# One Griffin/PEER decoder layer on one core: the mixers in two passes of 160 and 384 columns instead of one of 544

## The chip, the core and the metric

The kernel runs on one core of a Trainium2 chip. The metric is the device time of one execution in microseconds (us). Five engines take part: TensorE (PE, with its weight loads shown apart as PEld), VectorE (DVE), ScalarE (ACT), GpSimd (POOL) and SyncE (SP, which only issues DMAs). Each works through its own instructions in their order and waits at semaphores for the others.

## The reference

One layer is computed for 512 prompt tokens and 8 sequences of 4 sampled tokens, 544 tokens in all, with width 2048, in float32.

```python
def decoder_layer(x, ple, ...):
    n1 = rmsnorm(x, norm_mix)
    xr, gr, q, k, v, ga, gb = split(n1 @ w_in)            # 2048 -> 7680 columns
    xr, conv_new = causal_conv(xr, conv_buf, conv_w, conv_b)
    hr, h_last = rglru(xr, h0, ...)                        # linear recurrence over the tokens
    branch_a = (hr * gelu(gr)) @ w_proj_rnn
    o = attention over a window of 128 keys, with sinks    # q, k normed and rotated
    branch_b = o @ w_proj_attn
    x = x + (sigmoid(ga) * branch_a + sigmoid(gb) * branch_b) @ w_out
    x = x + peer(rmsnorm(x, norm_ffn), w_peer_q, peer_sub_keys, peer_u, peer_v)
    x = x + (ple @ w_ple) * sigmoid(rmsnorm(x, norm_ple) @ w_ple_gate)

def peer(x, w_q, sub_keys, u, v):     # 16384 experts, 8 heads, 16 experts of each head
    s = scores of (x @ w_q) against 2 x 128 sub-keys per head
    idx, g = softmax of the 16 best sums of the two top-16 lists
    h = gelu(x . u[idx]) * g
    return sum over the 128 chosen experts of h * v[idx]
```

A prompt token's recurrence and attention read only earlier prompt tokens; a sampled token reads only its own sequence's cache and state.

## The kernel before

Activations lie with the model dimension on the 128 partitions and tokens along the row: sixteen tiles of 128 x 544. A matmul has 128 x 128 weights and streams the tokens' columns. The work is a list of *units*: one unit is one 512 KB block of weights (8 tiles of 128 x 128). SP loads it (`wr`), ACT rounds it to a high part `wh` (line 230), DVE computes the rest `wl` (line 231), and PE multiplies, for each of the 8 tiles, `wh` by the high and the low part of the activations and `wl` by the high part: 24 products, each with a weight load of its own. With 544 columns each product is two matmuls of 272 columns (line 290), 48 matmuls a unit; with 384 columns it is one (line 286), 24 a unit.

The units come in this order: 4 for `w_ple`; the **mixers**, 120 for `w_in`, 32 for the two projections, 32 for `w_out`, 32 for `w_pq`, all with 544 columns (216 units); 256 for `u` and 256 for `v` with 384 columns; 32 for `w_gate` with 544.

PEER is done in two ways. The first 384 prompt tokens are done **densely**: all 16384 experts are multiplied (stages U and V), with a gate matrix `Gd` that is zero for experts not chosen. It is built in stage U: `tk1` and `tk2` find the top 16 on DVE, then `place` makes gate tiles with f16 matmuls (line 996) that ACT writes out (lines 1001, 1003). The other 160 tokens, the last prompt block and the samples, are done **sparsely**: their experts' rows are fetched by indirect DMAs issued on POOL (line 1076), 160 of `u` and 160 of `v`, 1 MB each, and DVE does a dot product (line 1089) or a scaled addition (line 1097) with each.

Such side work lives in generators that `side()` advances twice per unit, at a pace that the `PACE_...` constants set; so all engines' orders are fixed when the program is built. Some places call `drain()`, which issues all that is left of them at once. One is `gates_done`, 24 units before the end of stage U, where the gate matrix has to be complete: all that stage U's pace has not yet issued of `tk1`, `tk2` and `place` is put there, ahead of the next unit.

Of the kernel before, what the change touches and what calls it, by code (L numbers as in the profile page):

```python
# [17 lines left out]
P = 128  # L18
# [6 lines left out]
LP = 568  # L25
LH = LP // 2
RN = 8
# [3 lines left out]
NS = P + NSB  # L31
# [12 lines left out]
PACE_U, PACE_V = (1.3, 0.36), (1e6, 0.40)  # L44
NWA = min(NW - 4, 2 * KT * T // (2 * DC))
# [12 lines left out]
TT = _token_tiles(DC, T) + _token_tiles(0, DC)  # L58
# [10 lines left out]
def _build(ctx, tc, nc, I, O):  # L69
# [16 lines left out]
    xr_t = [None] * KT  # L86
    rawf = act.tile([P, KT * T], F32, name="raw")
    raw = rawf.rearrange("p (k t) -> p k t", k=KT)
    opf = act.tile([P, 2 * KT * T], F32R, name="opf")
    misc = act.tile([P, KT * NS + 3 * DC], F32, name="misc")  # L90
# [5 lines left out]
    ident = const("ident", [P, P])  # L96


    AH, AL = [None] * KT, [None] * KT

    def act_tile(k):
        return opf[:, 2 * k * T:(2 * k + 1) * T], opf[:, (2 * k + 1) * T:(2 * k + 2) * T]
# [17 lines left out]
    def sq_add(k, pool, x=0):  # L120

        new = x not in ssum
        if new:
            ssum[x] = 0, T, misc[:, (4 + x) * T:(5 + x) * T]
        s = ssum[x][2] if new else pool.tile([P, T], F32, name="sq", tag=f"sq{x}", bufs=2 - x)
        if x:
            GP.tensor_mul(s, raw[:, k, :], raw[:, k, :])
        else:
            A.activation(s, raw[:, k, :], AF.Square)
        if not new:  # L130
            (GP if x else V).tensor_add(ssum[x][2], ssum[x][2], s)

    def make_rs(keep):
        yield
        ps = psum.tile([P, 2, 512], F32, name="aux", tag="aux", bufs=2)
        for s in range(2):
            lo, hi = s * HB, (s + 1) * HB
            cut = sorted({lo, hi} | {c for c0, c1, _ in ssum.values() for c in (c0, c1) if lo < c < hi})
            for x, y in zip(cut, cut[1:]):
                qs = [q[:, x - c0:y - c0] for c0, c1, q in ssum.values() if c0 <= x and y <= c1]  # L140
# [4 lines left out]
        rs = keep[0] = cst.tile([P, T], F32, name="rs", tag="rs", bufs=1)  # L145
        A.activation(two(rs), ps[:, :, :HB], AF.Sqrt, bias=eps_t, scale=1.0 / D)
        V.reciprocal(rs, rs)


    LOADA, SPLITA = 4, 2  # L150
    pace = dict(main=1e6, sp=0.0)
    owed = dict(main=0.0, sp=0.0)

    def side():

        SPS["tick"] = SPS.get("tick", 0) + 1
        owed["sp"] += pace["sp"]
# [4 lines left out]
        while owed["main"] > 0:  # L162
            c, more = advance()
            owed["main"] -= c
            if not more:
                break

# [7 lines left out]
    def gemm(src, ops, epi, nk=2, cols=None, **kw):  # L175

        key = object()
        for hc in range(nk):
            last = hc == nk - 1
            unit(src(hc), [(key, [(kl, (lambda k=hc * 8 + kl: ops(k))) for kl in range(8)], hc == 0, last,  # L180
# [35 lines left out]
    def run_units():  # L216
        rawt, hit, lot = {}, {}, {}
        n = len(units)

        def load(u):  # L220
            if u < n:
                rawt[u] = wgt.tile([P, 8, P], F32, name="wr", tag="wr", bufs=3)
                SP.dma_start(out=rawt[u], in_=units[u]["src"])
# [9 lines left out]
        for u in range(LOADA):  # L233
            for k in ((0, 4, 8, 12) if u == LOADA - 1 else ()):
                SP.dma_start(out=raw[:, k:k + 4, :], in_=I["xT"][k:k + 4].rearrange("k p t -> p k t"))
                if k == 0:
                    load(u)
            if u < LOADA - 1:
                load(u)
        for u in range(SPLITA):  # L240
            split(u)
        for u in range(n):
# [5 lines left out]
            load(u + LOADA)  # L248
# [53 lines left out]
    def act_ops(k):  # L302
        return AH[k], AL[k]


    pa = ExitStack()
    pG = pa.enter_context(tc.tile_pool(name="pG", bufs=1))
    pA = None
    pl = ExitStack()
    pL = pl.enter_context(tc.tile_pool(name="pL", bufs=1))  # L310

    def aconst(pool, name, shape):
        t = pool.tile(shape, F32, name=name)
        SP.dma_start(out=t, in_=I[name])
        return t

    rs1 = [None]

    def start_a():
        for _ in range(N0A):  # L320
            yield
        for k in range(KT):
            AH[k], AL[k] = act_tile(k)
            split_to(AH[k], AL[k], raw[:, k, :], gn[:, 0, k:k + 1])
            if k < NPS:
                sq_add(k, pL, 1)
# [1179 lines left out]
```

## Time and profile before

| | us |
|---|---|
| median of 3 runs (4072.27 to 4082.82) | 4072.59 |
| profiled execution, its time | 4068.44 |
| its span, first to last instruction | 4066.6 |
| PE busy in the span | 3917.9 |
| DVE busy | 2694.7 |
| ACT busy | 1300.6 |
| POOL busy | 535.9 |

The profiled execution's own time is 1.84 us above its span. PE is busy for 96% of the span, but the end of a matmul is modelled and neighbours overlap, so this share does not say how fast the matmuls follow each other; that is read from the starts in the timeline or from a piece of the chain with its count. The granted TensorE clock is 0.979 of full speed as a mean.

### The profile page before, as it was taken

The numbers are of one execution on the slowest core, as the hardware profiler recorded it, in microseconds if no ns is written. First come the engines' busy times: TensorE is split into PE (matmuls) and PEld (weight loads), VectorE is DVE, ScalarE is ACT, GpSimd is POOL, SyncE is SP. The second block draws the span as 40 slices with busy tenths as digits, with TensorE's granted clock in tenths as the row PEclk, the third lists the DMA queues.
The fourth block names the chain that finished last, engine by engine and source line by source line (L and its number), as shares of the span: only waits on it lengthen the run. The fifth ranks groups of instructions, "written<-read, shape, count | busy, mean of one in ns | idle before, by whom it ended". The sixth has DMA issues, their size and how long they took to land.

```text
span 4066.6 us, 62629 instructions
## 1 busy us (share of the span) xinstructions
PE 3917.9 (96%) x26069; PEld 3847.3 (95%) x26069; DVE 2694.7 (66%) x3782; ACT 1300.6 (32%) x1653; POOL 535.9 (13%) x486
## 2 busy tenths in 40 slices
PE   7999999999999999999999998289999999999999
PEld 7999999999999999999999998289999999999999
DVE  7765445333434348998788987857788889578543
ACT  4442344421223223333333233133222323233421
POOL 3000000000000001222222221001222222013000
PEclk9999999999999999999999999599999999999999
DMA  5232232234333336998999998268999999689342
GB/s 189 79 113 95 74 101 92 93 101 147 131 130 116 114 110 228 332 334 325 335 339 327 332 331 316 90 228 314 345 366 383 362 358 376 234 283 365 124 136 99
DMA packets 324620, 909.47 MB, mean 224 GB/s; under 512 B 27496, under 2 KB 163624, under 8 KB 283248
## 3 DMA queue, kind: packets, MB, share of 16 engines
q1 hardware_dynamic: 201008, 489.54, 35.2%
q0 software_dynamic: 54400, 363.36, 23.5%
q10 hardware_dynamic: 68928, 52.57, 3.9%
q8 instruction: 204, 3.34, 0.3%
q14 instruction: 80, 0.66, 0.0%
HBM read 824.74 MB, written 80.63 MB: 223 GB/s over the span
## 4 chain that ended last, share of the span: by engine, by line
PE 72%; DVE 14%; DMA 8%; issue 3%; ACT 2%; SPq 1%; ACTq 1%; POOL 0%; DVEq 0%; POOLq 0%
PE acc L290 37%; PE acc L286 30%; DMA wr<-i_v 6%; DVE wl L231 4%; DVE raw L1097 2%; ACT wh L230 1%; DVE raw L1089 1%; DMA Gd<-gst 1%; PE aux L996 1%; DVE gb L1089 1%; ACTq L1150 1%; SPq L1178 1%; PE aux L525 1%; PE aux L562 1%; DVE gt L1182 0%
## 5 line engine op out<-in xcount | busy, mean ns | idle before, releaser
L286 PE MATMUL acc<-opf,wh 128*128 128x384 f32 x7424 | 1903.8, 337 | 4.2 <-ACT wh L230 4.1
L231 DVE TENSOR_TENSOR wl<-wr,wh 128x1024 fp32r<-128x1024 f32 x764 | 933.9, 1223 | 1175.7 <-ACT wh L230 1166.9
L290 PE MATMUL acc<-opf,wh 128*128 128x272 f32 x7936 | 1341.1, 291 | 22.9 <-ACT wh L230 9.7
L230 ACT ACTIVATE wh<-wr 128x1024 fp32r<-128x1024 f32 x764 | 804.9, 1059 | 1698.2 <-PE acc L290 772.3
L286 PEld LDWEIGHTS acc<-opf,wh 128*128 128x128 f32 x7424 | 1340.8, 188 | 7.2 <-ACT wh L230 7.2
L286 PE MATMUL acc<-opf,wl 128*128 128x384 f32 x3712 | 1247.5, 336 | 9.2 <-DVE wl L231 8.9
L290 PEld LDWEIGHTS acc<-opf,wh 128*128 128x128 f32 x7936 | 1132.7, 189 | 36.5 <-issue 14.1
L290 PE MATMUL acc<-opf,wl 128*128 128x272 f32 x3968 | 823.8, 289 | 0.0
L286 PEld LDWEIGHTS acc<-opf,wl 128*128 128x128 f32 x3712 | 697.7, 188 | 17.2 <-DVE wl L231 16.9
L290 PEld LDWEIGHTS acc<-opf,wl 128*128 128x128 f32 x3968 | 622.9, 189 | 0.3 <-DVE wl L231 0.3
L1097 DVE SCALAR_TENSOR_TENSOR raw<-gb,hsp,raw 128x2048 f32<-128x2048 f32 x96 | 225.0, 2343 | 1.8 <-DMA gb<-i_vn,idx 1.8
L1089 DVE SCALAR_TENSOR_TENSOR raw<-raw,misc 128x2048 f32<-128x2048 f32 x95 | 216.7, 2281 | 0.0
L1076 POOL DMA_INDIRECT raw<-i_un,idx x95 | 140.7, 1481 | 485.9 <-DVE raw L1097 274.0
L286 PE MATMUL acc<-wx,wh 128*128 128x384 f32 x768 | 196.9, 337 | 5.8 <-ACT wh L230 5.7
L1076 POOL DMA_INDIRECT gb<-i_vn,idx x97 | 128.7, 1326 | 539.8 <-DVE gb L1089 389.0
L1149 ACT ACTIVATE misc<-misc 128x384 f32<-128x384 f32 x128 | 67.4, 526 | 404.4 <-DVE misc L1148 404.4
L1089 DVE SCALAR_TENSOR_TENSOR gb<-gb,misc 128x2048 f32<-128x2048 f32 x65 | 148.3, 2282 | 0.0
L286 PEld LDWEIGHTS acc<-wx,wh 128*128 128x128 f32 x768 | 139.4, 189 | 7.4 <-ACT wh L230 7.4
L1097 DVE SCALAR_TENSOR_TENSOR raw<-raw,hsp 128x2048 f32<-128x2048 f32 x62 | 145.3, 2343 | 0.0
L1076 POOL DMA_INDIRECT gb<-i_un,idx x65 | 81.6, 1255 | 478.3 <-DVE raw L1097 240.5
L286 PE MATMUL acc<-wx,wl 128*128 128x384 f32 x384 | 130.3, 339 | 4.1 <-DVE wl L231 3.9
L1076 POOL DMA_INDIRECT raw<-i_vn,idx x63 | 87.2, 1383 | 286.2 <-DVE raw L1089 272.6
(302 smaller groups left out, 2316.4 us busy)
## 6 DMA issues: line engine op xcount, KB each, us to landing
wr<-i_u SPq DMA_DIRECT2D x256, 512.0 KB
wr<-i_v SPq DMA_DIRECT2D x256, 512.0 KB
wr<-i_w_in SPq DMA_DIRECT2D x120, 512.0 KB
Hd<-misc ACTq DMA_DIRECT2D x128, 192.0 KB
Gd<-gst ACTq DMA_DIRECT2D x12, 2048.0 KB
gt<-Gd SPq DMA_DIRECT2D x32, 768.0 KB
misc<-Hd SPq DMA_DIRECT2D x112, 192.0 KB
wr<-i_w_proj SPq DMA_DIRECT2D x32, 512.0 KB
```

Source lines behind the costliest of these rows:

```text
L230: A.activation(hit[u], r, AF.Copy)
L231: V.tensor_sub(lot[u], r, hit[u].bitcast(F32))
L286: PE.matmul(acc[:, 0, :ncol], lhsT=w[:, kl, :], rhs=x[:, :ncol], start=st and t == 0, stop=sp and t == 2)
L290: PE.matmul(acc[:, s, :HB], lhsT=w[:, kl, :], rhs=x[:, s * HB:(s + 1) * HB], start=st and t == 0, stop=sp and t == 2)
L525: PE.matmul(sc[:, g, j0:], lhsT=raw[hs, RN + 4 * kp + g, blk * P:(blk + 1) * P], rhs=Q["k", kp][hs, ks:ks + nk], start=True, stop=True)
L562: PE.matmul(ps[hs, 0, :], lhsT=Q["v", kp][:, blk - 1 + kb, hs], rhs=pt[:, kb, :], start=kb == kbs[0], stop=kb == 1)
L996: PE.matmul(pq[:, q], lhsT=oo[:, q // 2, 0, :, q % 2], rhs=gl[:, q // 2, x, :, q % 2], start=x == 0, stop=x == 1)
L1076: GP.indirect_dma_start(out=t, out_offset=None, in_=I[kind + "n"], in_offset=bass.IndirectOffsetOnAxis(ap=idx[:, i:i + 1], axis=0))
L1089: V.scalar_tensor_tensor(t, t, 1.0, xtok, op0=ALU.mult, op1=ALU.mult, accum_out=hsp[:, i:i + 1])
L1097: V.scalar_tensor_tensor(vacc, t, hsp[:, i:i + 1], vacc, op0=ALU.mult, op1=ALU.add)
L1149: A.activation(h, h, AF.Gelu_apprx_tanh)
L1150: A.dma_start(out=Hd[e], in_=h)
```

## The change

The tokens are put in the order: prompt blocks 1 to 3 (384 columns), prompt block 0 (128), samples (32). The 216 mixer units are run twice. **Pass A** does prompt block 0 and the samples, 160 columns; **pass B** does blocks 1 to 3, 384 columns, with the keys, values, convolution rows and recurrence state of block 0 kept from pass A. Each pass has its 216 units of weights loaded, split and multiplied, 24 matmuls a unit. The sparse tokens are now those of pass A. Their top-16 work runs as a background generator (`bg`) during the end of pass A and the start of pass B, and the rows of their experts are fetched during pass B and stage U (`u` rows) and during stages U and V (`v` rows; a `v` row may be fetched once pass B's scores are done). Stage U's side work keeps only the top-16 work and the placing of the three dense blocks. In pass A the weights of `w_in` are loaded into a ring of six buffers in memory that pass B's activations use later. Stages U, V and `w_gate` have the same matmuls as before.

```diff
-NS = P + NSB
+NA = P + NSB
+DB = T - NA
+NC = 0
+NS = NA + NC
 DC = T - NS
...
-PACE_U, PACE_V = (1.3, 0.36), (1e6, 0.40)
-NWA = min(NW - 4, 2 * KT * T // (2 * DC))
+PACE_A, PACE_U, PACE_V = 0.26, (1.35, 0.27), (1e6, 0.38)
+PACE_T = 1.2
...
-TT = _token_tiles(DC, T) + _token_tiles(0, DC)
+TT = _token_tiles(DB, T) + _token_tiles(DC, DB) + _token_tiles(0, DC)
+TA = 2
+TS = len(TT) - len(_token_tiles(0, DC))
...
+    PA, PB_ = Pass(), Pass()
+    for S, c0, n, npr, blk, ns, lp in ((PA, DB, NA, P, 0, NSB, 184), (PB_, 0, DB, DB, 1, 0, DB)):
+        S.c0, S.n, S.npr, S.blk, S.ns, S.lp = c0, n, npr, blk, ns, lp
...
+        def load():
+            u = nld[0]
+            if units[u].get("ring"):
+                r = u % RING
+                rawt[u] = rawf[:, r * 1024:(r + 1) * 1024].rearrange("p (k m) -> p k m", k=8)
+            else:
+                rawt[u] = wgt.tile([P, 8, P], F32, name="wr", tag="wr", bufs=WRB)
+            SP.dma_start(out=rawt[u], in_=units[u]["src"])
...
+    def split_b():
+        for k in range(8):
+            split_raw(PB_, (k,), 0)
+            yield
...
+        def win(epi):
+            gemm(wsrc("w_in", c[0]), S.ops, epi, cols=S.n)
...
+        for n in range(RN):
+            win(lambda a, n=n: (epi_xr(S, n, a), gens.append(lru(S, n))))
+            win(lambda a, n=n: epi_gr(S, n, a))
...
+        def post_lru():
+            flush()
+            drain()
+            if S is PB_:
+                while bg:
+                    bg_step()
...
+                X["t"] = [pX.tile([P, D], F32, name=f"xr{i}") for i in range(2)]
+                SPS["slots"] = SPS["slots"] + X["t"]
...
+            if S is PA:
+                open_l(PB_)
+                lru_consts(PB_)
+                TP["st"] = ExitStack()
+                TP["p"] = TP["st"].enter_context(tc.tile_pool(name="pT", bufs=1))
+                TP.update(eq=1, w=32, skl=None, sc=None)
+                pace.update(bg=PACE_T)
+                gens.append(rs_and_x())
+                return
...
+        if S is PA:
+            for u in units[start:start + 120]:
+                u["ring"] = True
...
+    def first_b():
+        drain()
+        split_raw(PB_, range(8, 16), 0)
+        gens.append(decay_rate(PB_))
+        maxact[0] = 2
+        sdiv[0] = 1.0
+        pace.update(sp=PACE_A)
...
+        q = j // 4
+        if S is PA:
+            if j % 4 == 3:
+                gens.append(scores(S, q))
+                bg.extend((tk1(0, q), tk2(0, 2 * q, 2)))
+            if j == KT - 1:
+                bg.extend((tk1(1, 0), tk2(1)))
+            return
...
+    seq = us[:P] + [("xtok", 0)] + us[P:P + PB]
...
+        seq += vs[:P]
+    seq += [("enda", 0)] + vs[P:P + PB]
...
+            if kind == "v" and ("scores", 3) not in PB_.done:
                 return
...
+    sa = mixers(PA)
+    units[sa]["pre"] = first_a
+    sb = mixers(PB_)
+    units[sb]["pre"] = first_b
+    weave_at(sb)
```

PE around a gate matmul of the recurrence, in the first part of the mixers. `wh` and `wl` are the weights, `opf` (and `opA` in pass A) the split activations, `x2` or `x4` the number of matmuls in a row. Before:

```order
L290 MATMUL acc<-opf,wh 128x272 x4
L290 MATMUL acc<-opf,wl 128x272 x2
L397 MATMUL aux<-xc,wrg 128x284 x2
L290 MATMUL acc<-opf,wh 128x272 x4
L290 MATMUL acc<-opf,wl 128x272 x2
```

The same place in pass A, and after the dots in pass B:

```order
L344 MATMUL acc<-opA,wh 128x160 x2
L344 MATMUL acc<-opA,wl 128x160
L484 MATMUL aux<-xc,wrg 128x184
L344 MATMUL acc<-opA,wh 128x160 x2
...
L344 MATMUL acc<-opf,wh 128x384 x2
L344 MATMUL acc<-opf,wl 128x384
L484 MATMUL aux<-xc,wrg 128x384
L344 MATMUL acc<-opf,wh 128x384 x2
```

Six matmuls of 272 columns for one weight tile have become three of 160 in one pass and three of 384 in the other.

DVE in the recurrence part of the mixers, between the splits (`wl`) of two units; `rec`, `r`, `ig`, `xc` belong to the recurrence. Before:

```order
L231 TENSOR_TENSOR wl<-wr,wh 128x1024
L422 TENSOR_SCALAR rec<-r 128x568
L423 RECIPROCAL rec<-rec 128x568
L426 TENSOR_TENSOR ig<-ig,xc 128x568
L428 COPY xc<-ig 128x1
L429 SCALAR_TENSOR_TENSOR r<-r,rec 128x568
```

In pass B of the change, where `eq`, `pk`, `hf` belong to the top-16 work of the sparse tokens and line 1307 is the dot product with a fetched row:

```order
L292 TENSOR_TENSOR wl<-wr,wh 128x1024
L468 TENSOR_TENSOR xp<-acc,rs 128x384
L493 TENSOR_SCALAR xc<-xp,cw,cb 128x384
L495 SCALAR_TENSOR_TENSOR xc<-xp,cw,xc 128x384 x3
L1141 TENSOR_TENSOR eq<-iota,hf 128x512
L1144 TENSOR_TENSOR eq<-eq,x1f 128x512
L1146 TENSOR_REDUCE pk<-eq 128x32
L292 TENSOR_TENSOR wl<-wr,wh 128x1024
L508 TENSOR_SCALAR rec<-r 128x384
L509 RECIPROCAL rec<-rec 128x384
L512 TENSOR_TENSOR ig<-ig,xc 128x384
L1307 SCALAR_TENSOR_TENSOR raw,hsp<-raw,misc 128x2048
```

The top-16 instructions, which stood in stage U, have moved between the splits of pass B's recurrence.

ACT near `gates_done`, late in stage U: `gst<-aux` takes a placed gate tile out of PSUM, `Gd<-gst` writes it out, `wh<-wr` is the split for a unit, `Hd<-misc` the result of an expert block. Before, with the last rows ahead of the next unit:

```order
L230 ACTIVATE wh<-wr 128x1024
L1001 ACTIVATE gst<-aux 128x128x8 x2
L1003 DMA Gd<-gst 128x32x128
L1001 ACTIVATE gst<-aux 128x128x8 x4
L1003 DMA Gd<-gst 128x32x128
...
L955 ACTIVATE pk<-pk 128x128
L977 ACTIVATE pkT<-aux 128x384
...
L1003 DMA Gd<-gst 128x32x128
L230 ACTIVATE wh<-wr 128x1024
```

In the change, around its last `Gd` write:

```order
L291 ACTIVATE wh<-wr 128x1024
L1208 ACTIVATE gst<-aux 128x128x8
L291 ACTIVATE wh<-wr 128x1024
L1373 ACTIVATE misc<-misc 128x384
L1374 DMA Hd_223<-misc 128x384
L1208 ACTIVATE gst<-aux 128x128x8
L1210 DMA Gd<-gst 128x32x128
L291 ACTIVATE wh<-wr 128x1024 x2
```

Before, 400 of the 768 placing matmuls, the whole third dense block among them, stand in one piece between two units at `gates_done`; in the change the last of them stands 11 units ahead of that place, and none is left there.

## Rows read from the trace of the kernel before

**Rows 1.** The page, part 1: busy us (share of the span), instructions.

```profile
PE 3917.9 (96%) x26069; PEld 3847.3 (95%) x26069; DVE 2694.7 (66%) x3782; ACT 1300.6 (32%) x1653; POOL 535.9 (13%) x486
```

**Rows 2.** Windows by stage; columns are named in the first row.

```profile
core 0: us, PE busy (x) PEld busy (x) DVE busy (x) ACT busy (x) POOL busy (x), PEclk, DMA share, GB/s
0.00:53.00 53.00, 30.28 (x192) 29.32 (x192) 41.95 (x37) 26.98 (x37) 36.77 (x31) 0.90 0.78 282
53.00:267.00 214.00, 213.77 (x1630) 210.49 (x1631) 149.75 (x251) 92.91 (x99) 5.71 (x34) 0.99 0.26 83
267.00:904.00 637.00, 637.00 (x4801) 605.34 (x4801) 280.82 (x369) 228.54 (x387) 25.05 (x45) 0.99 0.29 95
904.00:1508.00 604.00, 600.42 (x4755) 596.62 (x4754) 242.59 (x412) 152.65 (x179) 19.40 (x36) 1.00 0.38 126
1508.00:2769.00 1261.00, 1161.44 (x6974) 1141.22 (x6975) 1043.92 (x1727) 408.98 (x480) 233.10 (x166) 0.95 0.81 289
2769.00:3867.00 1098.00, 1081.47 (x6185) 1071.09 (x6185) 857.07 (x886) 341.93 (x417) 207.70 (x160) 1.00 0.87 321
3867.00:4066.60 199.60, 193.56 (x1541) 193.27 (x1539) 78.62 (x104) 48.57 (x56) 8.19 (x15) 0.99 0.35 119
```

**Rows 3.** The chain that ended last, two pieces: start us, us, what.

```profile
111.64 21.09 PE acc L290 x168
1763.37 82.08 PE acc L286 x466
```

**Rows 4.** Timeline of PE, short matmuls: start us, us, instruction.

```profile
457.12 1.91 PE L552 MATMUL aux<-ident,pr 128*128 128x128 f32 x16
3769.93 3.88 PE L1132 MATMUL aux<-tsel,raw 128*128 128x32 f32 x32
3773.62 0.99 PE L286 MATMUL acc<-opf,wh 128*128 128x384 f32 x2
1881.43 0.64 PE L996 MATMUL aux<-gl,oo 128*128 128x128 f16 x8
```

**Rows 5.** Lines' instructions, weight loads and matmuls: count, ns min/median/max, first and last start.

```profile
L286 PEld LDWEIGHTS acc<-opf,wh x7424: 186/188/333, 1507.9 to 3866.1; 128*128 128x128 f32 x196
L1132 PEld LDWEIGHTS aux<-tsel,raw x32: 188/192/337, 3769.8 to 3773.3; 128*128 128x128 f32 x32
L1132 PE MATMUL aux<-tsel,raw x32: 192/276/402, 3769.9 to 3773.4; 128*128 128x32 f32 x32
L996 PEld LDWEIGHTS <-oo x768: 96/97/149, 1881.4 to 2662.9; 128*128 128x128 f16 x192
L996 PE MATMUL aux<-gl,oo x768: 218/221/312, 1881.4 to 2663.0; 128*128 128x128 f16 x192
```

**Rows 6.** Windows late in stage U, line 286's instructions alone: PE, PEld, clock, DMA.

```profile
2508.00:2558.00 50.00, 15.03 (x83) 14.11 (x82) 0.73 0.70 227
2558.00:2608.00 50.00, 0.00 (x0) 0.00 (x0) 0.50 0.17 53
2608.00:2658.00 50.00, 0.00 (x0) 0.00 (x0) 0.57 0.42 126
2658.00:2708.00 50.00, 43.44 (x241) 42.55 (x242) 0.94 0.80 269
```

**Rows 7.** Window of the recurrence, line 231 alone: DVE busy, clock, DMA.

```profile
53.00:267.00 214.00, 40.33 (x33) 0.99 0.26 83
```

**Rows 8.** Groups on DVE: count, busy us, mean ns, idle before.

```profile
L1089 DVE SCALAR_TENSOR_TENSOR raw<-raw,misc 128x2048 f32<-128x2048 f32 x95 | 216.7, 2281 | 0.0
L944 DVE TENSOR_TENSOR eq<-iota,hf 128x512 f32<-128x512 f32 x34 | 23.2, 682 | 0.0
L871 DVE MAX8 v<-scp 128x8 f32<-128x128 f32 x68 | 19.0, 279 | 2.7 <-DMA scp<-scd 2.7
L873 DVE MAX8 ts<-cs 128x8 f32<-128x80 f32 x34 | 8.3, 245 | 1.2
L932 DVE SCALAR_TENSOR_TENSOR pk<-mk,hf 128x32 f32<-128x32 f32 x1 | 0.2, 184 | 0.0
L110 DVE SCALAR_TENSOR_TENSOR opf<-raw,gnorm,opf 128x544 fp32r<-128x544 f32 x32 | 38.5, 1268 | 1.3 <-ACT opf L109 1.3
L110 DVE SCALAR_TENSOR_TENSOR opf<-misc,gnorm,opf 128x160 fp32r<-128x160 f32 x16 | 6.1, 379 | 0.0
```

More of the change, by code (lines that the diff above doesn't have):

```diff
@@ L24 @@
 HB = T // 2
-LP = 568
-LH = LP // 2
 RN = 8
@@ L144, in make_rs @@
         ssum.clear()
[L145 to L152, printed above, removed]
+        for s, (lo, hi) in enumerate(parts):
+            A.activation(rs_t[:, lo:hi], ps[:, s, :hi - lo], AF.Sqrt, bias=eps_t, scale=1.0 / D)
+        V.reciprocal(rs_t[:, c0:c1], rs_t[:, c0:c1])
+    WRB = 4
+    LOADA, SPLITA = 5, 2
+    RING = 6
+    pace = dict(main=1e6, sp=0.0, bg=0.0)
+    owed = dict(main=0.0, sp=0.0, bg=0.0, side=0.0)
+    sdiv = [1.0]
+    bg = deque()
     def side():
         SPS["tick"] = SPS.get("tick", 0) + 1
+        owed["side"] += 1
+        if owed["side"] < sdiv[0]:
+            return
+        owed["side"] -= sdiv[0]
         owed["sp"] += pace["sp"]
@@ L166, in side, with bg_step @@
                 break
+        owed["bg"] = min(owed["bg"] + pace["bg"], 2 * pace["bg"])
+        while bg and owed["bg"] > 0:
+            owed["bg"] -= bg_step()
+    def bg_step():
+        try:
+            c = next(bg[0])
+            return 0.5 if c is None else c
+        except StopIteration:
+            bg.popleft()
+            return 0.1
     units = []
@@ L218, in run_units @@
         n = len(units)
[L220 to L223, printed above, removed]
+        nld = [0]
+        def load():
[6 more added lines that the diff above has]
+            SP.dma_start(out=rawt[u], in_=units[u]["src"])
+            nld[0] += 1
         def split(u):
@@ L231, in split @@
                 V.tensor_sub(lot[u], r, hit[u].bitcast(F32))
[L233 to L239, printed above, removed]
+        for u in range(3):
+            load()
+        load_x(PA)
         for u in range(SPLITA):
@@ L247, in run_units @@
                 flush()
-            load(u + LOADA)
+            while nld[0] < n and nld[0] <= u + (SPLITA + RING - 1 if units[nld[0]].get("ring") else LOADA):
+                load()
             split(u + SPLITA)
@@ L1101, in sp_step @@
         cost = 0.0
-        while fl and fl[0][0] not in "uv":
+        while fl and fl[0][0] not in "uv" and not SPS["hold"]:
             sp_use()
+        if SPS["tick"] < SPS["rest"]:
+            return cost
         if fl and not SPS["hold"] and SPS["tick"] - fl[0][3] >= TKD:
@@ L1246, in post_u @@
         drain()
-        assert not fl
-        for w in (14, 15):
+        while fl:
+            SPS["tick"] += 1
+            sp_step()
+            drain()
+        for w in range(12, 16):
             wsplit(w)
@@ L1264, in _build @@
     units[-24]["pre"] = gates_done
+    units[-40]["pre"] = lambda: SPS.update(slots=[x for x in SPS["slots"] if not any(x is y for y in X["t"])])
+    units[-10]["pre"] = lambda: SPS.update(pause=True)
     units[-4]["post"] = wsecond
```

888 lines of the change are left out of this document (514 added, 374 removed).

## The prediction, written before the changed kernel was run

> **What bounds the kernel now.** I began with the busy times of the page [rows 1]: PE has work for 3917.9 of 4066.6 us, DVE for two thirds, and no other engine for more than a third. So PE's instruction stream sets the time, and the first question is how fast its matmuls follow each other. The windows by stage [rows 2] cut the span into the start (53 us), the mixers (214 + 637 + 604 = 1455), U (1261), V (1098) and `w_gate` (199.6). The reader is to see three things there. In the mixers PE has no idle time (0.23, 0 and 3.58 us). In U it has 100 us. In U and V the DMA share is 0.81 and 0.87 at 289 and 321 GB/s, while the mixers take 83 to 126 GB/s.
>
> The chain that ended last [rows 3] gives the pace of the two shapes: 21.09 us for 168 matmuls of 272 columns, 125.5 ns each; 82.08 us for 466 of 384 columns, 176.1 ns each. Between the two lie 112 columns and 50.6 ns, 0.452 ns a column. That line, carried down to 160 columns, gives 125.5 - 112 x 0.452 = 74.9 ns. Whether a matmul of 160 columns runs on that line is what decides this change.
>
> The idle time of U has one place. Line 286, U's main matmul, hardly runs between 2508 and 2708 us [rows 6]: PE busy with it is 15.03, 0, 0 and 43.44 us in four windows of 50, so 141.5 us are missing. This is the lump at `gates_done`, where the third dense block's top-16 and placing stand ahead of the next unit.
>
> **The change, part by part.** *The mixers' matmuls.* Removed: 216 units x 48 = 10,368 matmuls of 272 columns, x 125.5 ns = 1301.2 us. Added: 216 x 24 = 5184 of 384 columns, x 176.1 = 912.9 us, and 5184 of 160 columns. The columns streamed are the same, but each weight tile now serves 160 of them in pass A, and each matmul has its own weight load (26069 of both [rows 1]). No row of the trace has 160 columns with rounded operands. Short f32 matmuls with full weights are the nearest [rows 4]: 16 of 128 columns take 1.91 us; less the 0.28 us that the last of them is drawn with (the median of line 1132's, [rows 5]), that is 15 steps of 109 ns. And 32 of only 32 columns, line 1132, take 3.88 us, (3.88 - 0.40)/31 = 112 ns; by their first and last starts, 3769.9 and 3773.4 [rows 5], the steps are 113. So from 32 to 128 columns the pace does not move: it is not the columns that set it. The f16 matmuls of 128 columns go at (0.64 - 0.22)/7 = 60 ns [rows 4, 5], and their weight loads last 97 ns against 192 for line 1132 and 188 for line 286 [rows 5]. So the step follows the weight load, and the rounded weights of line 286 load like the f32 ones. I therefore take 112 ns for 160 columns, against 74.9 from the line: 5184 x 112 = 580.6 us. The term is 912.9 + 580.6 - 1301.2 = **+192** us. Its ends are the line's 74.9 ns (388.3 us, term 0) and the 125.5 ns of the next longer shape (650.6 us, term +262).
>
> [...]
>
> *The mixers' other PE work* (attention, recurrence gates, transposes) is 1455 - 1301 = 154 us and has the same columns in all: 0.
>
> *The recurrence of pass B.* DVE did 149.75 us in the 214 us of the recurrence [rows 2], 40.33 of it splits, 1.22 each [rows 7]; the other 109.4 are 8 heads at 13.7 us. With 384 columns for 568 or 544 a head is some 9.7 us, as a fixed part stays: 78 us. Added are 32 splits again (39) and the top-16 pieces of the sparse tokens: four pieces of two heads, each of 20 instructions at 0.28, 10 at 0.24, 6 at 0.68 and some 35 short ones at 0.18 [rows 8], 18.4 us, 74 in all; and 7 dots of 2.28 [rows 8], 16, with 2 for the decay rate. Together 209 us. PE has 32 x 24 x 0.1761 = 135 us there and about 15 for gates (before: 214 - 32 x 48 x 0.1255 = 21 at 544 columns), 150. The `wl` splits stand behind the top-16 work on DVE, so PE waits for them. That is 59 us if DVE never pauses, and less for what DVE carries past the stage into the following units, where it is a third to half busy. I take **+48**; ends 20 and 70.
>
> *The recurrence of pass A.* PE has 32 x 24 x 0.112 + 6 = 92 us, DVE 39 + 8 heads at a third of the columns (about 46) = 85, ACT nearly its 92.91 [rows 2], since half of that is splits and fixed cost. Three engines of equal load that hand to each other do not reach the sum of any: **+12**, ends 0 and 30.
>
> *The start.* Line 110 makes the first activations, 16 times 1.27 us at 544 columns and 0.38 at 160 [rows 8]: 14 us less on DVE; and 3.1 MB of `x` less must land first, at 282 GB/s [rows 2] 11 us, beside it. **-16**, ends -25 and 0.
>
> *Stage U.* Nothing is drained at `gates_done` any more, so the 141.5 us go; but the 400 placing matmuls of that lump still run on PE, 400 x 60 ns = 24 us. **-118**, ends -141 and -90 (part of the third block's DVE work then makes a split late elsewhere).
>
> *Hand-overs between the parts of the mixers* (`w_in` to projections, to `w_out`, to `w_pq`, and pass A to B) happen twice. They cost 3.8 us of PE idle now [rows 2]; a second set with half the matmuls a unit to cover it: **+8**, ends 0 and 25.
>
> *Stage V* has 16.5 us of PE idle [rows 2], and about half of its fetched rows and scaled additions go to U: **-5**, ends -9 and 0.
>
> *At nothing:* loading and splitting the weights twice. A unit of pass A lasts 24 x 0.112 = 2.7 us; DVE's split is 1.22 of that, and 0.52 MB in 2.7 us is 195 GB/s, under the 321 of V [rows 2]. In pass B a unit of 4.2 us takes 124 GB/s and some 99 rows of 1 MB in 913 us take 115 more, 239 together. Without that cover a unit of pass A could be no shorter than 0.52 MB at 321 GB/s, 1.6 us, still below 2.7.
>
> **Sum:** 192 + 48 + 12 - 16 - 118 + 8 - 5 = +121 us on the profiled execution's 4068.44, so 4190. That execution is 4.1 us (0.1%) below the median of the runs; I leave this out. The likeliest's own range is 4130 to 4250. A measurement here tells some 0.3% (12 us) from no change.
>
> **The rivals.** *B, the weight load is hidden.* Pass A's matmuls run on the line at 75 to 79 ns. For it: the rows of 109 to 113 ns are bursts of 16 and 32, most with operands that are not rounded, and line 286 hides its loads of 188 ns. Against it: 32 and 128 columns at one pace, and f16 at 60 ns. The mixers' term falls by 5184 x 35 ns = 181 us; then pass A's recurrence waits for DVE and ACT, some +22. 4190 - 181 + 22 = about 4030, faster. It decides from 112 - 121/5.184 = 88.7 ns on: below that pace the change gains. [...]
>
> *C, the clock falls.* After line 1132 the next two matmuls of line 286 take 0.99 us [rows 4], several times their pace; and where PE had little to do at `gates_done` the clock was granted at 0.50 [rows 6]. [...] If pass A with its short matmuls were granted that, a step would take at least 160 columns at twice 0.452 ns, 145 ns: 5184 x 33 ns = +171 us, 4360, and more if the weight loads stretch too. Against it: PE never stops in pass A, and the recurrence had 0.99 [rows 2].
>
> *D, U keeps its wait.* The top-16 work of three dense blocks and 134 row operations remain in U; if DVE is late with its splits there in many small waits, the 118 us come back in part: about 4290. Against it: DVE has 1043.92 of 1261 us now [rows 2], and loses the sparse block's top-16.
>
> **How the numbers follow.** The likeliest has 0.80, B 0.11, C 0.04, D 0.05. Range 4110 to 4280: it leaves out B, C and D's upper part; its lower end is the likeliest with the start, the drain and pass B's recurrence all at their good ends, its upper end with the mixers' term 60 up or with pass B's stall and the hand-overs at their bad ends. Faster 0.10 (nearly all of B), same 0.03 (B's part with a pace near 88.7 ns), slower 0.87.
>
> **What would show it.** Right: a piece of the chain of pass A's w_out or w_pq units at 108 to 116 ns a matmul; pass A's projections to w_pq at a clock near 1.0; DVE over 90% busy in pass B's recurrence with PE waiting for `wl`; no window of U without its main matmul; stage U near 1145 us. Wrong: a pace below 89 ns in pass A; idle time of PE in pass A that ends on DMA; U still above 1220 us.

## The result, and the profile after

The changed kernel takes 4667.53 us (median of 4 runs, 4657.86 to 4676.77) against 4074.45: a ratio of 1.1451, interval 1.1418 to 1.1484. The forecast was 4190 with a range to 4280. Slower was right, the size was not: the loss is 593 us instead of 121. The profiled execution took 4660.96 us with a span of 4659.2. Nearly the whole error lies in one stage, and the cause stands in one column of the profile.

The page of the changed kernel: busy time of PE, DVE and ACT as in [rows 1], and PE and its granted clock in 40 slices of 116 us.

```profile
PE 4524.9 (97%) x26067; PEld 4444.5 (95%) x26067; DVE 2998.1 (64%) x4438; ACT 1612.7 (35%) x2112; POOL 570.6 (12%) x552
...
PE   8999999999789999999999999999999999999999
...
PEclk7655555557889999999999999999999999999999
```

PE has as many instructions as before and is busy all the time, yet for the first ten slices its clock is granted at 0.5 to 0.7. The windows by stage of the changed kernel (they answer to [rows 2]): start, pass A, the recurrence of pass B, the rest of pass B, U, V, `w_gate`.

```profile
core 0: us, PE busy (x) PEld busy (x) DVE busy (x) ACT busy (x) POOL busy (x), PEclk, DMA share, GB/s
0.00:36.00 36.00, 26.07 (x191) 25.55 (x192) 21.51 (x36) 17.68 (x30) 17.97 (x31) 1.00 0.94 334
36.00:1146.00 1110.00, 1092.07 (x5625) 1081.39 (x5624) 440.06 (x837) 373.51 (x549) 42.62 (x101) 0.56 0.38 121
1146.00:1360.00 214.00, 157.36 (x799) 146.84 (x797) 187.35 (x501) 94.78 (x114) 12.43 (x24) 0.89 0.35 117
1360.00:2244.00 884.00, 856.45 (x4784) 822.16 (x4783) 651.91 (x879) 338.21 (x479) 159.39 (x160) 0.99 0.71 249
2244.00:3387.00 1143.00, 1127.96 (x6940) 1104.24 (x6939) 922.47 (x1340) 396.09 (x469) 209.66 (x137) 1.00 0.85 295
3387.00:4472.00 1085.00, 1083.81 (x6297) 1083.38 (x6296) 703.72 (x757) 350.85 (x428) 120.34 (x84) 1.00 0.72 252
4472.00:4659.00 187.00, 181.18 (x1444) 180.96 (x1442) 71.11 (x93) 41.55 (x45) 8.22 (x15) 0.99 0.35 117
```

Pass A's clock is 0.56 as a mean, and PE is busy for 1092 of its 1110 us: it does not wait much, it is slow. By the stages' first matmuls, against the forecast's terms:

| | forecast, us | measured, us | off by |
|---|---|---|---|
| start | 37 | 36.4 | -1 |
| pass A (581 + 45 + 12 + 4) | 642 | 1109.1 | +467 |
| pass B (913 + 109 + 48 + 4) | 1074 | 1098.7 | +25 |
| U | 1141 | 1143.2 | +2 |
| V to the end | 1295 | 1271.8 | -23 |

V and `w_gate` came out 23 us shorter than forecast; V's idle time of PE fell from 16.5 to 1.2 us, where the forecast took 5, and the rest was not followed. Of pass B's 25 us, 4 are the top-16 term (e7_no_top16, below), and the rest was not followed either.

The timeline of PE in pass A of the changed kernel, at 600 us: start, us, instruction.

```profile
599.62 0.63 PE L344 MATMUL acc<-opA,wh 128*128 128x160 f32 x2
600.05 0.41 PE L344 MATMUL acc<-opA,wl 128*128 128x160 f32 x1
600.26 0.63 PE L344 MATMUL acc<-opA,wh 128*128 128x160 f32 x2
```

Three matmuls start from 599.62 on and the next three from 600.26, 0.64 us later: 213 ns each, with no idle time between. This is at a clock of 0.50 (window 596 to 606). Of the 1110 windows of 1 us from 36 to 1146, 979 are at 0.50 and 123 at 1.00, so pass A has other stretches too. Four windows of 6 us of the changed kernel (us, PE, PEld, DVE, ACT and POOL busy, clock, DMA share, GB/s):

```profile
132.00:138.00 6.00, 6.00 (x54) 6.00 (x54) 5.69 (x21) 5.94 (x9) 0.58 (x4) 0.96 0.05 20
...
156.00:162.00 6.00, 5.64 (x51) 5.48 (x50) 5.66 (x21) 4.83 (x7) 0.28 (x2) 1.00 0.55 175
162.00:168.00 6.00, 2.45 (x10) 2.24 (x11) 5.83 (x13) 3.96 (x5) 0.29 (x3) 0.60 0.12 25
168.00:174.00 6.00, 6.00 (x29) 6.00 (x29) 4.63 (x14) 2.34 (x3) 0.30 (x2) 0.50 0.71 233
```

From 132 to 162 us the clock is at or near 1.00 and 54 matmuls fit in 6 us, 111 ns each, the forecast's price. At 168 the same matmuls are back at 29 in 6 us. What lies between, in the timeline of PE:

```profile
161.14 0.39 PE L344 MATMUL acc<-opA,wh 128*128 128x160 f32 x2
161.37 0.27 PE L344 MATMUL acc<-opA,wl 128*128 128x160 f32 x1
163.80 0.72 PE L344 MATMUL acc<-opA,wh 128*128 128x160 f32 x2 [2.16 <-ACT wh L291]
```

One wait of 2.16 us for a split. Ahead of the scores pass A falls to 0.50 four times and stays there for about 85, 215, 157 and 515 us. The first three falls come with waits of PE of 1.59, 2.16 and 2.09 us. The fourth, which opens the longest stretch, comes without one. Two windows of PE around that place (us, PE busy, clock, DMA share, GB/s) and its timeline; lines 723 and 724 are small matmuls of the attention:

```profile
556.00:576.00 20.00, 20.00 (x163) 0.92 0.52 167
576.00:596.00 20.00, 20.00 (x103) 0.50 0.18 58
```

```profile
569.91 0.29 PE L723 MATMUL aux<-spt,vc 128*64 128x16 f32 x2
570.13 0.28 PE L724 MATMUL aux<-spn,vn 32*64 32x16 f32 x2
...
572.72 0.36 PE L724 MATMUL aux<-spn,vn 32*64 32x16 f32 x2
573.02 0.40 PE L723 MATMUL aux<-spt,vc 128*64 128x16 f32 x2
```

Here 32 instructions of 16 columns stand in a row, and the clock falls during them with PE busy for 20.00 of 20.00 us: the steps go from 0.22 us (569.91 to 570.13) to 0.32. The kernel before has the same row twice, at 810 and 818 us, and there the clock falls without a wait too (0.50 from 815 to 817 and from 821 to 827). But behind it come matmuls of 272 columns, and from 829 on the clock is back at 1.00.

And where the clock of the changed kernel rises again, near the end of pass A:

```profile
1085.70 0.63 PE L344 MATMUL acc<-opA,wh 128*128 128x160 f32 x2
1086.34 1.99 PE L1054 MATMUL aux<-skl,raw 128*128 128x128 f32 x8
...
1088.47 0.39 PE L344 MATMUL acc<-opA,wh 128*128 128x160 f32 x2
1088.69 0.27 PE L344 MATMUL acc<-opA,wl 128*128 128x160 f32 x1
1088.80 0.39 PE L344 MATMUL acc<-opA,wh 128*128 128x160 f32 x2
```

Behind a row of f32 matmuls (the scores) the same stream goes on at half the step: 1088.47 to 1088.80 for three, 111 ns.

**Theory L:** the clock falls, mostly at a wait of PE, as it did in the kernel before (waits of 6.39 us ahead of 53.23 and of 2.09 us ahead of 1311.03); but behind a fall the matmuls of 160 columns stay at 0.50, here for up to 515 us, until some other work comes. In the mixers of the kernel before, each fall was followed by 272 columns, and the clock was back at 1.00 within 10 us (at 57, 829 and 1317 us). **Rival W:** the short pass's waits and hand-overs hold the clock down, whatever the width. **Rival S:** the stream of 160 columns is granted 0.50 in itself, so a rise cannot last. A second question is what gave U its 118 us, which the forecast got right by reasoning about the lump at `gates_done` alone.

### The profile page after: what moved, and what is told of

The parts are those of the page before. It is cut to its first block, busy times and chain, and to the rows that moved or that the text cites. A ratio compares the mean times of both kernels' runs of the same rounds, so it can differ in the third digit from the quotient of the medians.

```text
span 4659.2 us, 64983 instructions
## 1 busy us (share of the span) xinstructions
PE 4524.9 (97%) x26067; PEld 4444.5 (95%) x26067; DVE 2998.1 (64%) x4438; ACT 1612.7 (35%) x2112; POOL 570.6 (12%) x552
## 4 chain that ended last, share of the span: by engine, by line
PE 60%; DVE 7%; ACT 1%; issue 1%; DMA 1%; ACTq 0%; SPq 0%; DVEq 0%
PE acc L344 53%; PE acc L348 4%; DVE wl L292 2%; PE aux L1203 1%; DVE raw L1315 1%; DMA skl<-i_skT 1%; DVE xr L1307 1%; DVE raw L1307 0%; ACT wh L291 0%; PE aux L665 0%; ACTq L1374 0%; PE aux L631 0%; DVE misc L1372 0%; PE aux L1054 0%; DVE scr L1067 0%
## 5 line engine op out<-in xcount | busy, mean ns | idle before, releaser
L344 PE MATMUL acc<-opf,wh 128*128 128x384 f32 x10240 | 2633.5, 338 | 3.1 <-DVE opf L142 1.7
L344 PEld LDWEIGHTS acc<-opf,wh 128*128 128x128 f32 x10240 | 1850.9, 189 | 23.3 <-issue 11.8
L344 PE MATMUL acc<-opf,wl 128*128 128x384 f32 x5120 | 1720.0, 336 | 20.1 <-DVE wl L292 19.9
L344 PE MATMUL acc<-opA,wh 128*128 128x160 f32 x3456 | 1004.9, 393 | 2.3 <-ACT wh L291 2.2
L344 PEld LDWEIGHTS acc<-opf,wl 128*128 128x128 f32 x5120 | 965.2, 189 | 30.9 <-DVE wl L292 30.9
L344 PEld LDWEIGHTS acc<-opA,wh 128*128 128x128 f32 x3456 | 873.6, 309 | 6.2 <-issue 2.9
L344 PE MATMUL acc<-opA,wl 128*128 128x160 f32 x1728 | 675.1, 391 | 1.9 <-DVE wl L292 1.9
L344 PEld LDWEIGHTS acc<-opA,wl 128*128 128x128 f32 x1728 | 533.1, 308 | 2.3 <-DVE wl L292 2.3
L344 PE MATMUL acc<-wx,wh 128*128 128x384 f32 x1408 | 357.2, 334 | 0.0
L1307 DVE SCALAR_TENSOR_TENSOR xr<-xr,misc 128x2048 f32<-128x2048 f32 x86 | 196.4, 2283 | 0.0
```

What stands on the lines that cost most here:

```text
L344: PE.matmul(acc[:, 0, :ncol], lhsT=w[:, kl, :], rhs=x[:, :ncol], start=st and t == 0, stop=sp and t == 2)
L1307: V.scalar_tensor_tensor(t, t, 1.0, xtok, op0=ALU.mult, op1=ALU.mult, accum_out=hsp[:, i:i + 1])
```

## The experiments on pass A

**e1_wide256: 256 columns instead of 160.** The operand lies in memory beside its neighbours, so the moving side is only read further.

```diff
-                        PE.matmul(acc[:, 0, :ncol], lhsT=w[:, kl, :], rhs=x[:, :ncol],
+                        nx = 256 if ncol == NA else ncol
+                        PE.matmul(acc[:, 0, :nx], lhsT=w[:, kl, :], rhs=x[:, :nx],
```

> Pass A's matmuls stream 256 columns instead of 160: 96 more that nobody reads, the neighbouring operand's. More work per matmul, the same number of matmuls and weight loads. Theory L (the low clock is kept by the narrow stream: a wait of PE lets the clock fall to 0.50, and matmuls of 160 columns do not bring it back): pass A is granted about 1.0, a matmul of 256 columns lies on the line at 125.5 - 16 x 0.452 = 118 ns, 5184 of them take 612 us, pass A some 690 in place of 1109, the whole 4200 to 4300 us. Rival W (the waits and hand-overs of the short pass hold the clock down, whatever the width): the clock stays at 0.50, 256 columns take at least 231 ns, the whole 4750 us or more.

Measured: 4276.34 us, ratio to before 1.0491 (1.0474 to 1.0509). Sixty per cent more columns in pass A make the changed kernel 391 us faster. The windows of this run, all of pass A and then line 347 (its matmuls) alone in a stretch without waits:

```profile
37.00:762.00 725.00, 688.63 (x5622) 673.65 (x5622) 437.14 (x837) 367.53 (x549) 43.42 (x101) 0.97 0.56 185
```

```profile
607.00:637.00 30.00, 30.00 (x257) 30.00 (x256) 1.00 0.67 212
```

The clock is 0.97, a step is 30/257 = 117 ns (the line gives 118), and pass A takes 725 us instead of 1110, close to the 690 of theory L. The waits are still there, 36 us of PE idle, and the clock still falls: of the 23 windows of 30 us from 37 to 727, eight lie below 1.00. But the lowest of them has 0.83, some 10 of its 30 us at 0.50 if the rest is at 1.00; so W falls.

**e2_bursts: pass A as it is, with dense work thrown in.** Ahead of every third unit 8 f32 matmuls of two constants (16 instructions in the trace).

```diff
+            if U.get("cols") == NA and u % 3 == 0:
+                ps = psum.tile([P, 2, 512], F32, name="aux", tag="aux", bufs=2)
+                for i in range(8):
+                    PE.matmul(ps[:, 0, :P], lhsT=ident, rhs=ones, start=True, stop=True)
```

> The changed kernel with work added: ahead of every third unit of pass A, 8 f32 matmuls of 128 columns whose result nobody reads (72 bursts, the form of the scores' matmuls after which the clock rose at 1088 us). Pass A's own matmuls stay at 160 columns. Theory L: after each burst the clock is 1.0 and stays until PE next waits some 2 us; the stages without waits run at 111 ns a matmul; bursts cost 72 x 0.9 to 1.9 us; the whole 4240 to 4400 us. Rival S (a stream of 160 columns is granted 0.50 in itself, also where PE never waits): the clock falls again right after each burst, the whole is 4660 plus the bursts, 4730 to 4800 us.

Measured: 4370.9 us, ratio 1.0728 (1.0711 to 1.0746): 297 us faster than the changed kernel, by adding 1152 instructions to the busiest engine. Windows of all of pass A, and of a stretch with the projections and `w_out`:

```profile
37.00:857.00 820.00, 790.81 (x6772) 780.39 (x6772) 438.13 (x836) 368.25 (x548) 43.00 (x101) 0.96 0.49 164
517.00:697.00 180.00, 180.00 (x1611) 179.74 (x1610) 100.84 (x164) 75.33 (x110) 6.32 (x12) 1.00 0.60 200
```

1611 matmuls in 180 us, 112 ns each, at a clock of 1.00. S, which had this run above 4730, falls.

**e5_four_bursts: the same burst only four times.** It tells for how long one burst is good.

```diff
+            if u in (70, 126, 158, 190):
+                ps = psum.tile([P, 2, 512], F32, name="aux", tag="aux", bufs=2)
...
```

> The changed kernel with only four bursts of 8 f32 matmuls of 128 columns, ahead of pass A's units 70, 126, 158 and 190: behind the keys and queries, and two units into the projections, w_out and w_pq. Theory L (the low clock is kept by the stream until something denser comes, the high one until PE waits): from each burst to the next wait a matmul takes 111 instead of 213 ns, up to 24 x 0.102 = 2.4 us a unit; over some 90 to 130 units, 220 to 300 us less: 4360 to 4450 us. Rival S (the stream by itself is granted 0.50): the clock is back at 0.50 a few us after each burst, 4640 to 4680 us.

Measured: 4502.47 us (4497.26 to 4550.32), ratio 1.1053 (1.1031 to 1.1074). That is 165 us less than the changed kernel, and less of a gain than I expected (220 to 300). Windows at the second burst and at the end of its effect, and the two places in the timeline of PE:

```profile
680.00:700.00 20.00, 20.00 (x150) 20.00 (x150) 9.68 (x17) 6.95 (x9) 0.00 (x0) 0.82 0.71 235
...
880.00:900.00 20.00, 20.00 (x97) 19.43 (x97) 5.37 (x6) 6.16 (x8) 2.00 (x4) 0.50 0.42 138
```

```profile
682.86 3.69 PE L315 MATMUL aux<-ones,ident 128*128 128x128 f32 x16
...
876.68 0.34 PE L348 MATMUL acc<-opA,wl 128*128 128x160 f32 x1 [1.74 <-DVE wl L292]
```

Behind the burst at 682.86 the clock is 1.00 (700 to 860), and it stays for some 190 us, until a wait of 1.74 us for a split behind the hand-over to `w_pq`. The first burst, at 366, lasted only to a wait of 2.09 us in the attention at 391 (1.00 up to 392, 0.50 from 394), and the fourth, at 861, stood ahead of the wait and could not help behind it. I had placed the bursts two units into each part, and the wait that matters came later.

The 190 us at 111 ns instead of 213 are worth 190 x 102/111 = 175 us, but the traced execution is the slowest of the five, 4550.32 us, and gained only 111 on the traced one of the changed kernel. One reason is in its timeline:

```profile
549.79 1.91 PE L661 MATMUL aux<-ident,pr 128*128 128x128 f32 x8
```

The same row of eight f32 instructions was followed by 1.00 in the changed kernel (at 552.39), and here it was not: the clock is 0.50 in each window of 20 us from 540 to 680. The scores' row of eight at 939 left the clock there too (0.50 from 880 to 1020). So not all other work was followed by 1.00, and the same row was in one execution and not in another. With 1.00 for the rest, the mean clocks (0.887 of 4659.2 us in the changed kernel, 0.911 of 4548.6 here) stand for an estimated 1053 and 810 us at 0.50. The 243 us less are worth 243 x 102/213 = 116 us, and pass A is 110 shorter (999 against 1109).

**e3_hi_lo_320: two wider matmuls in place of three.** High and low part of an activation lie side by side, so the high weights can take both at once.

```diff
+                if ncol == NA:
+                    PE.matmul(acc[:, 0, :2 * NA], lhsT=h[:, kl, :], rhs=al, start=st, stop=False)
+                    PE.matmul(acc[:, 0, :NA], lhsT=l[:, kl, :], rhs=ah, start=False, stop=sp)
...
+        A.activation(misc[:, o:o + NA], acc[:, 0, NA:2 * NA], AF.Copy)
+        V.tensor_add(acc[:, 0, :NA], acc[:, 0, :NA], misc[:, o:o + NA])
```

> In pass A the high weights are multiplied by high and low part of the activations in one matmul of 320 columns (they lie side by side), the low weights by the high part in one of 160: two matmuls and two weight loads a tile instead of three, and one copy and one addition more for each output tile. Theory L: 320 columns take 125.5 + 48 x 0.452 = 147 ns, 160 columns 111, 1728 x 258 = 446 us; with the denser stream the clock is near 1.0; pass A 520 to 560 us, the whole 4060 to 4120 us. If the wider stream does not bring the clock back after waits: 1728 x (290 + 213) = 869 us, the whole 4450 to 4550 us.

Measured: 4222.83 us, ratio 1.0357 (1.034 to 1.0374): the best of the two-pass kernels, but 100 to 160 us above what I expected. Windows of its recurrence and of all of pass A:

```profile
39.00:189.00 150.00, 115.33 (x726) 108.44 (x726) 113.22 (x275) 101.54 (x148) 9.85 (x39) 0.89 0.51 166
39.00:713.00 674.00, 571.22 (x3894) 541.81 (x3893) 472.31 (x961) 387.01 (x672) 43.57 (x101) 0.90 0.62 199
```

Pass A takes 674 us, 103 of them with PE idle, and the clock is 0.90. With two thirds of the matmuls a unit leaves less cover for its two splits and the additions; in the recurrence PE, DVE and ACT are busy for 115, 113 and 102 of 150 us. The mean of 0.90 stands for some 135 us at 0.50, if the rest is at 1.00. At 1.00 a matmul takes 0.134 us (222 in the 29.78 us that PE is busy from 549 to 579). At that pace the 3456 of pass A take 463 us, and its other work takes 45 by the forecast; PE is busy for 571, so the lower clock cost an estimated 60 us beside the 103 of idle time.

## The experiments on pass B, U and V

**e7_no_top16.** What the top-16 pieces cost in pass B; `no_top16` fills experts and gates with constants.

```diff
-                bg.extend((tk1(0, q), tk2(0, 2 * q, 2)))
...
-                bg.extend((tk1(1, 0), tk2(1)))
+                bg.append(no_top16())
```

> The changed kernel with the sparse tokens' top-16 work left out: every sparse token gets the same fixed experts with a fixed gate, so the fetches, dots and additions stay. It measures what the top-16 pieces cost in pass B's recurrence (the forecast's term of 48 us). If the forecast's mechanism holds (DVE is the bound there, 187 of 214 us, and PE's splits stand behind it): the first 214 us of pass B shrink to 150 to 170 us and the whole falls by 40 to 75 us, to 4590 to 4630. Rival: PE's waits there have other causes (the heads' own chain of DVE, ACT and PE), then less than 20 us.

Measured: 4608.27 us as the median of 4 runs, 59 less than the changed kernel. Three are 4607.94 to 4616.41; the fourth took 4515.45 at a mean clock of 0.910 against their 0.89, so in these four how long the clock was low differed between executions of one kernel; where it differed no trace shows. The traced one is of the three, and its pass A takes 1106 us against the changed kernel's 1109, so the two traces can be compared. Pass B takes 1047.1 instead of 1098.7 us: 51.6 less, where the forecast had 48. Its first 32 units, the recurrence, take 163 us instead of 214:

```profile
1143.00:1306.00 163.00, 149.73 (x800) 142.94 (x799) 128.66 (x196) 86.77 (x102) 11.97 (x26) 0.96 0.44 154
```

PE's largest wait in the first 214 us of pass B, of the changed kernel and then of this run (us in total, times, longest):

```profile
PE aux L484 <- DVE xc L495: 50.1, 7, 10.7
```

```profile
PE aux L484 <- DVE xc L495: 13.3, 6, 4.8
```

The size is the forecast's and DVE is the cause; the place is not quite: in the changed kernel PE waits at the gate matmul, whose input `xc` comes late from DVE, and only 3.4 us at the splits. Part of the size is the clock, which the forecast did not have there: in the recurrence it was granted at 0.89 in the changed kernel and at 0.96 here.

**e4_before_pace: the kernel before without its lump.** One number: `PACE_U` (1.3, 0.36) to (1.9, 0.36).

> The kernel before with one number changed: stage U's side work is issued at a pace of 1.9 instead of 1.3, so that the last gate tile is placed 48 units ahead of gates_done and nothing is drained there. It asks what of the change's gain in stage U needs the two passes. If the lump alone was lost time (the forecast's term of 118 us): 3950 to 3990 us. Rival: DVE, with 1044 us of work in U, becomes late with its splits in many small waits, and the time is 4030 to 4080 us.

Measured: 4109.17 us, ratio 1.0082 (1.0065 to 1.0099): 0.8% longer, and above both ranges. The window of U in this run, and PE's largest wait in it:

```profile
1512.00:2814.00 1302.00, 1186.18 (x6959) 1144.65 (x6960) 1045.24 (x1727) 402.94 (x480) 223.08 (x166) 0.97 0.80 281
```

```profile
PE acc L286 <- DVE wl L231: 72.5, 60, 3.4
```

The lump is gone and U takes 1302 us, 43 more than the 1259 between the same two matmuls of the kernel before. The wait is spread over 60 late splits, which cost 4.9 us in the kernel before; ahead of 49 of them (67.4 us) DVE had gone from one instruction to the next without a pause. So taking the lump apart is not by itself what the change gained by.

**e6_before_rows_later: less DVE work in U.** `PACE_U` (1.5, 0.28): no lump, and 35 row operations (159 less 124; the expectation says 36) move to V.

> The kernel before, one pass, with two numbers changed: stage U's side work at a pace of 1.5, the fetched rows at 0.28 instead of 0.36, so that 36 row operations of 2.3 us go from U to V and nothing is drained at gates_done (the last gate tile is placed 10 units ahead). Theory D (DVE's total in U decides: the change gained there because it took row operations and one token tile's top-16 out of U, 1044 us of DVE work): U loses 83 us of DVE work and falls by 60 to 100 us, V rises by 10 to 40; the whole 3990 to 4060 us. Rival P (it is the even spreading that costs, each top-16 piece makes a split late): as with the faster pace alone, 4090 to 4130 us.

Measured: 4055.38 us, ratio 0.9955 (0.9936 to 0.9974). Windows of U and V, and PE's largest wait in V:

```profile
1513.00:2697.00 1184.00, 1150.11 (x6963) 1120.23 (x6962) 963.78 (x1673) 402.73 (x479) 193.96 (x130) 1.00 0.79 277
2697.00:3851.00 1154.00, 1085.58 (x6190) 1076.49 (x6189) 935.42 (x940) 342.10 (x418) 264.54 (x195) 0.97 0.91 337
```

```profile
PE aux L1132 <- DVE raw L1097: 51.5, 1, 51.5
```

DVE's work in U falls by 79 us and U by 75, as theory D has it; the changed kernel, with 922 us of DVE work there, stands at 1143. V gives 54 back, in one wait for the last row addition. A run at (1.5, 0.36) was not made, so how much of the 75 us is the pace's alone stays open.

**e8_before_middle: between the two.** `PACE_U` (1.5, 0.32).

> The kernel before with stage U's pace at 1.5 and the fetched rows at 0.32: between the kernel before (159 row operations ahead of V, 400 placing matmuls drained at gates_done) and the run at 0.28 (124 and 0): 142 row operations and 96 placing matmuls. Theory D (what U gains by fewer row operations V pays back in part, here 75 us against 55): U some 40 to 60 us below the kernel before, V 25 to 35 above, the whole 4040 to 4065 us. Rival: the lump and the dense spreading both cost in part, and there is no gain between them: 4065 to 4090 us.

Measured: 4025.91 us, ratio 0.9885 (0.986 to 0.991), better than expected: U takes 1219 us and V does not rise at all.

```profile
1511.00:2730.00 1219.00, 1162.92 (x6963) 1131.10 (x6963) 1003.48 (x1700) 402.86 (x478) 218.70 (x148) 0.98 0.81 284
2730.00:3823.00 1093.00, 1080.85 (x6195) 1073.97 (x6194) 895.28 (x915) 342.95 (x418) 229.34 (x177) 1.00 0.91 339
```

**e10_before_v_faster and e11_before_v_more: can V take the rest?** `PACE_U` (1.5, 0.28) with `PACE_V` 0.45, and (1.5, 0.24) with 0.50.

> The kernel before with stage U as in the run at 1.5 and 0.28 (U 1184 us) and stage V's rows at a pace of 0.45 instead of 0.40. There V stood 51.5 us in one wait of PE for the last row addition. If the additions were only issued too late: that wait goes, V is 1100 us or a little less, the whole 3995 to 4015 us. Rival: the transfers cannot go faster (V's DMA share is 0.91 there) or DVE, then busy for more than 0.85 of V, makes the splits late: 4030 to 4060 us.

> As the run at 1.5, 0.28 and 0.45, with 16 more row operations moved from U to V (0.24 in U, 0.50 in V). If DVE's total goes on deciding in U and V has room: U 1150 to 1170 us, V up to 1120, the whole 3980 to 4015 us. If V is full (DMA share 0.9 at 337 to 339 GB/s already): V 1130 us or more and the whole above the run with 0.28.

Measured: 4060.15 us, ratio 0.9973 (0.9957 to 0.9989), and 4097.22 us, ratio 1.0062 (1.0045 to 1.0079). Windows of V and PE's largest wait in it, of the first and then of the second, and the window of U of the second:

```profile
2697.00:3851.00 1154.00, 1108.62 (x6211) 1092.32 (x6210) 938.54 (x944) 342.37 (x419) 252.25 (x195) 0.98 0.90 337
```

```profile
PE acc L286 <- ACT wh L230: 33.5, 14, 5.0
```

```profile
2692.00:3896.00 1204.00, 1124.90 (x6202) 1101.01 (x6201) 976.25 (x969) 342.23 (x418) 259.04 (x212) 0.96 0.90 338
```

```profile
PE acc L286 <- ACT wh L230: 63.9, 16, 6.4
```

```profile
1510.00:2692.00 1182.00, 1151.22 (x6961) 1122.12 (x6962) 929.15 (x1646) 405.24 (x478) 149.09 (x113) 1.00 0.75 262
```

The one wait at the end is gone, but V does not get shorter: it moves 337, 337 and 338 GB/s in e6, e10 and e11, and with more rows it only lasts longer, now with PE waiting for splits. Those splits were late for their weights' transfers: ACT itself had sat idle for the block's DMA ahead of 12 of the 14 (31.8 of the 33.5 us) and of 15 of the 16 (63.4 of the 63.9). So V has room for the 17 rows that e8_before_middle moves there, not for 35.

The gain in U that was expected of e11 (1150 to 1170 us) did not come either. It has 929 us of DVE work there against 964 in e6, and U takes 1182 us against 1184 (1193 in e10, built as e6 there). The changed kernel, with nearly the same DVE work as e11, 922 us, takes 1143. So DVE's total alone does not set U, and theory D is only part of the answer. PE waits for DVE's splits for 29.1 us in 33 pieces in e11, and for 12.1 in 19 in the changed kernel, whose U is without the sparse tokens' top-16 but has more row operations (134 against 105). What the rest of the 39 us is was not separated.

## Why the prediction was wrong

**The step that failed** is the first term: "I therefore take 112 ns for 160 columns". The pace is right at the clock for which the rows were read: 111 ns wherever pass A had 1.00, in the changed kernel and in e2_bursts. But all those rows came from a kernel in which 272 or 384 columns stood behind each fall of the clock in the mixers and behind line 1132, and the clock was back at 1.00 within 10 us (at 829 and 3778 us, for two). I carried their clock along with their pace. At 0.50 a step is 213 ns. With 5184 of them at 213 the term would have been 912.9 + 1104.2 - 1301.2 = +716 instead of +192. Not all of pass A was that slow: some 980 of its 1110 us were at 0.50 (mean clock 0.56), and 980 x 102/213 = 469 us is what they cost by an estimate, which agrees with the 467 measured. With these the 4190 become 4657.

**Rival C** named this mechanism, with a chance of 0.04 and 4360 us, "and more if the weight loads stretch too". They did: a load of line 344 lasted 309 ns as a mean in pass A and 189 with 384 columns. My argument against it was "PE never stops in pass A, and the recurrence had 0.99 [rows 2]". Both halves were poor. The forecast's own term for pass A's recurrence had three engines waiting for each other, and the longest fall needed no wait at all. From 400 to 700 us PE was busy for 300 of 300 us at a clock of 0.53, so busy time as the profile shows it did not tell the clock. And 0.99 was measured with 272 columns, behind which the clock came back. What [rows 4] showed, two matmuls of 384 columns in 0.99 us behind line 1132, was such a fall without a wait (0.50 from 3774 to 3776). It was about twice their time at 1.00 (0.18 + 0.34 us), not several times; what I did not ask is what it took to rise again. None of the signs that I had named for being wrong covered it.

**Right:** the start (-16.6 us against -16), the direction, that pass A's weights load in time (121 GB/s; PE's 8.5 us of waits on DMA are all for the scores' sub-keys), pass B's stall in size and engine (51.6 against 48, by e7_no_top16; by place and clock not quite), and the length of U (1143 against 1141).

**Right for an incomplete reason:** U. The forecast put its gain down to the lump. e4_before_pace took away only the lump and U became longer; e6_before_rows_later took away DVE work as well and U became 75 us shorter. The idle time at `gates_done` was in good part DVE's work gathered in one place, as a window of the kernel before shows (us, PE, PEld, DVE, ACT and POOL busy):

```profile
2558.00:2608.00 50.00, 1.39 (x3) 0.55 (x3) 45.59 (x204) 2.66 (x6) 0.00 (x0) 0.50 0.17 53
```

The changed kernel relieved DVE in U: it has 134 row operations there for 157, and the sparse tokens' top-16 went into pass A and pass B. e11_before_v_more shows that DVE's total is not the whole cause, so that the term came out within 2 us is in part luck.

**Rival B** (the line, 75 ns) and **rival D** (U keeps its wait) did not occur: no stretch of pass A's main matmuls was faster than 111 ns, and U took 1143 us.

No two-pass kernel came near the kernel before; the best is e3_hi_lo_320 with 4222.83. The kernel before with two paces changed, e8_before_middle, beats both at 4025.91.

## What to carry to other kernels

A pace read from these traces belonged to a granted clock (111 ns at 1.00, 213 at 0.50, both with 160 columns), and the clock to the stream around it (0.56 for pass A with 160 columns, 0.97 with 256). When a change makes a long stream of narrower matmuls, look in the trace at hand for every fall of the clock, at a wait or without one, and ask what ran until it rose again; if the new stream has nothing of the kind, price it at the lower clock. And the idle lump on PE was not a cost that went away when it was spread (U took 43 us more in e4_before_pace): look at whose work fills it, and move that work to a stage with room, as far as that stage's transfers allow.

## What the runs showed of the hardware that was not expected

- PE without idle time stayed at 0.50 in the changed kernel: 470 matmuls of 160 columns in the 100 us from 900 to 1000, 213 ns each. e5_four_bursts' rows of 16 f32 instructions at 366 and 682 (3.5 and 3.7 us) were followed by 1.00, which the second time held through 160-column matmuls for 190 us. Rows of 8 (1.9 to 2.0 us) were followed by 1.00 in the changed kernel at 376, 552 and 1086, and not in e5_four_bursts at 549 and 939.
- In pass A, waits of 2.16 us (at 163, the changed kernel) and of 2.09 and 1.74 us (at 393 and 876, e5_four_bursts) went with a fall to 0.50 within 4 us. A row of 32 instructions of 16 columns went with one too, with PE never idle (570 to 573 us, and 810 and 818 us in the kernel before).
- The step of the 160-column matmuls nearly doubled at the lower clock: 111 ns at 1.00, 213 at 0.50.
- Wider was faster: 256 columns at 117 ns (clock 1.00) against 160 at 213 (clock 0.50).
- Each f32 matmul of the bursts was two instructions in the trace (72 x 8 matmuls, 1152 instructions more).
